# Delta-rule stage of a hybrid encoder layer: values' convolution, q decays and gate product on GpSimd, one-strand substitution

## The chip, the core and the metric

The kernel runs on one core of one Trainium2 chip. Five engines work side by side, each through its own instruction stream in a fixed order: PE (TensorE, matrix products), DVE (VectorE), ACT (ScalarE), POOL (GpSimd) and SP (which issues most DMAs). Semaphores tie the streams together. The metric is the device time of one execution in microseconds. The kernel before takes 1628.24 us (median of 3 runs, 1626.96 to 1631.02).

## The reference, cut to what matters

One layer: a norm, one wide projection, two token mixers in parallel, gates, an output projection. The change lies in mixer A, the gated delta rule, with 8 heads of width 128 over 1024 tokens, in both directions.

```python
qkv_a = silu(centred_depthwise_conv(qkv_a, conv_w))      # 5 taps along the tokens, per channel
q_a, k_a, v_a = split(qkv_a, 3); q_a = l2norm(q_a); k_a = l2norm(k_a)
# gated_delta_rule, per head and direction, in chunks:
diff = g[..., :, None] - g[..., None, :]
decay = where(incl, exp(diff), 0)
lower = where(strict, einsum(kb, k) * decay, 0)          # kb = k * beta
u, w  = triangular_solve(I + lower, [v * beta, kb * exp(g)])
attn  = einsum(q, k) * decay; q_dec = q * exp(g); k_dec = k * exp(g_last - g)
for each chunk:                                          # the scan over chunks
    v_new = u - w @ S
    o     = q_dec @ S + attn @ v_new
    S     = S * exp(g_last) + k_dec.T @ v_new
o_a = rmsnorm(o_fwd + o_bwd) * silu(z_a)                 # z_a: a further part of the projection
```

## The kernel before, in words

**Stages.** First the tokens are normalised and split in two single-precision parts (`hh`, `hl`), so that each projection is three products. Then comes the delta-rule stage over heads h = 0 to 7, then mixer B (GLA, 4 heads), then the two mixer projections (`pj_y`) and the output projection (`pout`). The sixteen gate projections `t0` to `t15` are work for PE that may stand anywhere; thirteen are planned behind the last delta-rule head.

**One head of the delta-rule stage** has four parts:
- `gdn_project(h+1)`: PE computes k, q and v (`pj_a`) and the gate z (`pj_z`) of the next head. ACT copies each result into a padded buffer `xp` (2 of them). The 5-tap convolution is one product with a scalar (L517, for q on ACT at L515) and four multiply-adds on DVE (L519), each over 128x1024. SiLU on ACT follows (L500). z is copied out to DRAM (`z_d`) as it is.
- `gdn_decay(h+1)`: loads the decay exponents, masks them on POOL (L585), takes exponentials on ACT (L588).
- `gdn_inverse(h)`: products k k^T (`pgr`), scaled into `um` (L628). The 32x32 diagonal blocks are inverted by back substitution on DVE (L641 to L653): 31 steps, each a product into `tmp` (L651) and a subtraction from `yl` (L653), done in two strands (even and odd columns), so 4 instructions a step, 120 a head. Then PE joins the blocks (`p1`, `py`, `px`, `p2`, `p3`); the values are turned to token order and scaled (L731, on DVE); the q k^T products are multiplied by the decays (L740).
- `gdn_scan(h)`: 8 chunk steps in both directions, an alternation of small PE products and small DVE and ACT instructions (`r` L780, `vd` L786, `vn` L788, `S` L798, outputs `po` L767). Ahead of it the decays exp(g) are loaded into `qe` and multiplied by q (L749, DVE). Behind it come the norm, the product with silu(z) (`finish`, L472; the multiplication shows as L127 `zs`), two multiply-adds with PSUM (L476) and the store.

**What sets the order.** Instructions are recorded with priorities: the inverse of head h+1 ranks ahead of the scan of head h, the projections rank last and fill PE. A scheduler lays out each engine's stream once, by its own estimate of durations; on the chip every engine then takes its stream strictly in that order. POOL also computes the low parts `lo` of the weights (L184) on which the next projections wait.

**Buffers** in the stage: q 2, k 3, v 3 (`A_BUFS`), `xp` 2, `qe` 2 (used again for the output `o`), one `zs`.

Of the kernel before, what the change touches and what calls it, by code (L numbers as in the profile page):

```python
# [32 lines left out]

WRAW, WSPLIT, XS, XP = 2, 4, 4, 2

A_BUFS = (2, 3, 3)

# [53 lines left out]
def layer_kernel(  # L91
# [107 lines left out]
    for h in range(HA):  # L199
        plan += [(f"a{j}_{h}", w_in, [(j * D + h * P, P, 0)]) for j in A_ORDER]  # L200
        plan.append((f"z{h}", w_in, [(C_Z + h * P, P, 0)]))
        if h > 0:
            plan_gates(("gdn", h - 1), GDN_FILL[h - 1])
    plan_gates(("gdn", HA - 1), GDN_FILL[HA - 1])
    for h in range(HB):
# [192 lines left out]
    SC = [P, 2, HA, NT]  # L398
    be = mconst.tile(SC, F32, name="be")
    nb = mconst.tile(SC, F32, name="nb")  # L400
    ev = mconst.tile([P, 2, 3, HA, NT], F32, name="ev")
    nE = mconst.tile(SC, F32, name="nE")
    def scan_gates(pool):
# [44 lines left out]
        for d in range(2):  # L448
# [49 lines left out]
    def gdn_project(h, pool):  # L498
        a = [pool.tile([P, T], F32, tag=f"a{j}", name=f"{'qkv'[j]}{h}", bufs=A_BUFS[j]) for j in range(3)]
        silu = lambda t: tc.keep_in_program_order(nc.scalar.activation(t, t, AF.Silu))  # L500
        for j in A_ORDER:
            xp = pool.tile([P, T + 4], F32, tag="xp", name=f"xp{j}_{h}", bufs=XP)
            nc.gpsimd.memset(xp[:, 0:2], 0.0)
            nc.gpsimd.memset(xp[:, T + 2:T + 4], 0.0)
            evac = lambda th, ps: nc.scalar.copy(xp[:, 2 + th * 512:2 + th * 512 + 512], ps)
            if h == 0 and j == A_ORDER[0]:
                evac(0, ps_a[0])
                for i in range(2, 4):
                    a_steps[i]()
                evac(1, ps_a[1])  # L510
            else:
                project(f"a{j}_{h}", evac)
            ct = j * 8 + h
            if j == 0:
                nc.scalar.mul(a[j], xp[:, 0:T], cw[:, ct, 0:1])  # L515
            else:
                nc.vector.tensor_scalar(a[j], xp[:, 0:T], cw[:, ct, 0:1], None, op0=ALU.mult)  # L517
            for k in range(1, 5):
                nc.vector.scalar_tensor_tensor(a[j], xp[:, k:k + T], cw[:, ct, k:k + 1], a[j], op0=ALU.mult, op1=ALU.add)  # L519
            if h == 0 and j == A_ORDER[0]:  # L520
                table(SILU)
                silu(a[j])
                exp_ln_table()
        if h == 0:
# [3 lines left out]
            exp_ln_table()  # L528
            with at(P_FILL):
                project_out("z0", z_d[:, 0])  # L530
# [9 lines left out]
    zs = {}  # L540

# [49 lines left out]
    def gdn_inverse(h, pool, sm, qkv, dt):  # L591
        qT, kT, vT = qkv
        t2 = lambda n, shape: pool.tile(shape, F32, tag="t2", name=f"{n}{h}", bufs=4)
# [48 lines left out]
        for i in range(31, 0, -1):  # L642
            for par in range(2):
                s0 = (i // 2 + 1 - par) // 2
                w_ = 8 - s0
                if w_ == 0:
                    continue
                tmp = sm.tile([P, 31 * 8], F32, tag=f"tmp{par}", name=f"tmp{h}_{i}_{par}", bufs=1)
                tv = tmp[:, :i * w_].rearrange("p (r s) -> p r s", s=w_)
                yv = yl.rearrange("p r (s e) -> p e r s", e=2)[:, par, :, s0:]  # L650
                nc.vector.tensor_tensor(tv, ul2[:, i, 0:i].unsqueeze(2).broadcast_to([P, i, w_]),  # L651
                                        yv[:, i].unsqueeze(1).broadcast_to([P, i, w_]), op=ALU.mult)
                nc.vector.tensor_tensor(yv[:, 0:i], yv[:, 0:i], tv, op=ALU.subtract)  # L653
        yt = t2("yt", [P, 16, 32])
# [88 lines left out]
    def gdn_scan(h, pool, sm, qkv, dt, um, ktok, vtok, rk2, c2):  # L743
        qT, kT, _ = qkv
# [24 lines left out]
        for s in range(NT):  # L769
# [30 lines left out]
            for d, n in un:  # L800
# [3 lines left out]
                add_o(n, vn[d], dt[:, d * NT + n])  # L804
        if h == HA - 1:
            zs[h] = gdn_z(h, pool)
            table(SILU)
            tc.keep_in_program_order(nc.scalar.activation(zs[h], zs[h], AF.Silu))
            exp_ln_table()

# [7 lines left out]
    with tc.tile_pool(name="gdn", bufs=1) as pool, tc.tile_pool(name="gdns", bufs=2) as sm:  # L818
        scan_gates(pool)
        o128 = mconst.tile([P, P], F32, name="o128")  # L820
# [4 lines left out]
        for h in range(HA):  # L825
# [327 lines left out]
```

## Time and profile before

| | |
|---|---|
| median of 3 runs | 1628.24 us |
| profiled execution | 1627.11 us, span of its instructions 1624.2 us |
| busy share PE / DVE / ACT / POOL | 94% / 54% / 43% / 12% |
| mean granted clock of PE | 0.961 |
| the chain that ended last | PE 67%, DVE 16%, ACT 7%, DMA 6% |

The span divides at about 80 us and 845 us: start, delta-rule stage, everything later. Busy times are unions of the instructions' durations on an engine. A PE that reads busy is not PE at its peak, since matmuls are pipelined.

### The profile page before, as it was taken

Reading aid. Unit: us, or ns where it says so; the run is one execution under the profiler, and the core shown is the slowest. Engines: PE = TensorE matmul, PEld = TensorE weight load, DVE = VectorE, ACT = ScalarE, POOL = GpSimd, SP = SyncE. Lnnn points to the kernel's source line nnn. Section 1 sums busy time; section 2 is a strip of 40 time slices with the busy share of each in tenths; the row PEclk is TensorE's granted clock in tenths of the full one; section 3 lists DMA queues with packets and bytes.
Section 4 is the critical chain, followed back from the end, with each engine's and each line's share of the span. In section 5 each row is a group of like instructions: output and inputs, shape, how many; then the busy total and the mean of one; then the engine's idle time right before and its main releaser. Section 6 shows DMA issues by size and latency. Waiting matters only on the chain.

```text
span 1624.2 us, 25070 instructions
## 1 busy us (share of the span) xinstructions
PE 1531.2 (94%) x9500; PEld 1290.5 (79%) x9500; DVE 881.9 (54%) x2340; ACT 696.9 (43%) x1473; POOL 193.8 (12%) x207
## 2 busy tenths in 40 slices
PE   6978997998899999999989999999999999899998
PEld 6867776787777878778778888898888988787887
DVE  5486486877879897958541013313314245435413
ACT  5462443355364645543332234524525455424311
POOL 3211131112122121200000020020110100000000
PEclk9988996999999999989899999999999999999999
DMA  5320230112032221312234321131231335755404
GB/s 162 130 67 21 72 97 27 33 66 73 26 111 66 79 91 47 110 53 59 83 104 123 99 71 40 40 98 33 72 71 41 91 97 159 230 161 174 133 32 156
DMA packets 142562, 142.05 MB, mean 87 GB/s; under 512 B 11419, under 2 KB 115531, under 8 KB 141413
## 3 DMA queue, kind: packets, MB, share of 16 engines
q1 hardware_dynamic: 134546, 126.11, 25.9%
q10 hardware_dynamic: 7256, 12.26, 2.5%
q0 software_dynamic: 640, 2.10, 0.4%
q8 instruction: 74, 1.21, 0.3%
q14 instruction: 46, 0.38, 0.1%
HBM read 109.97 MB, written 30.46 MB: 86 GB/s over the span
## 4 chain that ended last, share of the span: by engine, by line
PE 67%; DVE 16%; ACT 7%; DMA 6%; issue 2%; SPq 2%; POOL 1%; DVEq 0%; ACTq 0%; POOLq 0%
PE pj_t L254 9%; PE pj_y L254 8%; PE pj_v L243 6%; PE pout L143 5%; PE pj_a L254 5%; PE pj_g L254 5%; DVE tmp L651 4%; DVE yl L653 4%; PE pj_k L254 3%; PE pj_z L254 3%; PE pj_q L254 2%; PE po L767 2%; PE psb L945 2%; PE pob L967 2%; PE psc L793 2%
## 5 line engine op out<-in xcount | busy, mean ns | idle before, releaser
L254 PE MATMUL pj_a<-hh,hi_a 128*128 128x512 f32 x368 | 154.5, 420 | 11.1 <-ACT gz L284 6.9
L254 PE MATMUL pj_a<-hl,hi_a 128*128 128x512 f32 x368 | 153.2, 416 | 0.0
L254 PE MATMUL pj_a<-hh,lo_a 128*128 128x512 f32 x368 | 152.5, 414 | 0.0
L254 PE MATMUL pj_t<-hh,hi_t 128*128 128x512 f32 x256 | 105.4, 412 | 0.0
L254 PE MATMUL pj_t<-hl,hi_t 128*128 128x512 f32 x256 | 105.0, 410 | 0.0
L254 PE MATMUL pj_t<-hh,lo_t 128*128 128x512 f32 x256 | 104.6, 408 | 0.0
L184 POOL TENSOR_TENSOR lo_a<-raw_a,hi_a 128x512 fp32r<-128x512 f32 x48 | 70.0, 1457 | 281.3 <-ACT hi_a L180 259.1
L788 ACT ACTIVATE vn<-psc,rk 128x128 f32<-128x128 f32 x128 | 45.2, 366 | 120.8 <-DVE vd L786 73.5
L651 DVE TENSOR_TENSOR tmp<-ulb,yl 128x54 f32<-128x54 f32 (+13 forms) x480 | 93.3, 234 | 1.8 <-DMA yl<-in_consts_dram 1.7
L254 PEld LDWEIGHTS pj_a<-hh,hi_a 128*128 128x128 f32 x368 | 72.9, 198 | 25.4 <-ACT gz L284 7.6
L653 DVE TENSOR_TENSOR yl<-yl,tmp 128x54 f32<-128x54 f32 (+13 forms) x480 | 90.9, 231 | 0.1
L254 PEld LDWEIGHTS pj_a<-hl,hi_a 128*128 128x128 f32 x368 | 72.5, 197 | 14.0 <-issue 0.7
L254 PEld LDWEIGHTS pj_a<-hh,lo_a 128*128 128x128 f32 x368 | 72.1, 196 | 13.8 <-issue 0.7
L254 PE MATMUL pj_y<-ob,hi_y 128*128 128x512 f32 x256 | 79.0, 390 | 1.3 <-DVE gb L1072 1.3
L143 PE MATMUL pout<-wo,hh 128*128 128x512 f32 (+1 forms) x272 | 79.7, 377 | 0.0
L243 PE MATMUL pj_v<-lo_v,hh 128*128 128x256 f32 x256 | 72.4, 283 | 0.0
L243 PE MATMUL pj_v<-hi_v,hl 128*128 128x256 f32 x256 | 72.4, 283 | 0.0
L243 PE MATMUL pj_v<-hi_v,hh 128*128 128x256 f32 x256 | 72.4, 283 | 0.0
L184 POOL TENSOR_TENSOR lo_v<-raw_v,hi_v 128x512 fp32r<-128x512 f32 x32 | 41.3, 1291 | 233.0 <-ACT hi_v L180 233.0
L180 ACT CAST hi_a<-raw_a 128x512 fp32r<-128x512 f32 x48 | 29.7, 620 | 67.0 <-PE pj_a L254 38.0
L143 PEld LDWEIGHTS pout<-wo,hh 128*128 128x128 f32 x272 | 50.1, 188 | 9.5
L793 PE MATMUL psc<-vd,ktok 128*128 128x128 f32 x224 | 47.2, 305 | 11.0 <-ACT vn L788 11.0
(315 smaller groups left out, 3993.1 us busy)
## 6 DMA issues: line engine op xcount, KB each, us to landing
raw_a<-in_w_in_dram SPq DMA_DIRECT2D x48, 256.0 KB
dt<-cr_d SPq DMA_DIRECT2D x8, 1024.0 KB
qe<-eg_d SPq DMA_DIRECT2D x16, 512.0 KB
raw_t<-in_w_in_dram SPq DMA_DIRECT2D x32, 256.0 KB
gt_d<-gt SPq DMA_DIRECT2D x64, 128.0 KB
raw_v<-in_w_in_dram SPq DMA_DIRECT2D x32, 256.0 KB
xt<-in_x_dram SPq DMA_DIRECT2D x8, 512.0 KB
raw_z<-in_w_in_dram SPq DMA_DIRECT2D x16, 256.0 KB
```

The lines of the kernel that those rows point to most:

```text
L143: nc.tensor.matmul(ps, lhsT=a(k), rhs=b(k), start=(s == 0), stop=(s == len(steps) - 1))
L180: i = nc.scalar.copy(hi, raw)
L184: nc.gpsimd.tensor_tensor(lo, raw, hi.bitcast(F32), op=ALU.subtract)
L243: nc.tensor.matmul(ps[b][:, c * 256:(c + 1) * 256], lhsT=a[th][:, kk, ts], rhs=w[:, k, :], start=kk == 0 and i == 0 and c == 0, stop=kk == ...
L254: nc.tensor.matmul(ps[:, cols], lhsT=a[:, k, :], rhs=b[th][:, kk, cols], start=kk == 0 and a is hi and b is src[0], stop=kk == KD - 1 and ...
L651: nc.vector.tensor_tensor(tv, ul2[:, i, 0:i].unsqueeze(2).broadcast_to([P, i, w_]), yv[:, i].unsqueeze(1).broadcast_to([P, i, w_]), op=ALU ...
L653: nc.vector.tensor_tensor(yv[:, 0:i], yv[:, 0:i], tv, op=ALU.subtract)
L767: nc.tensor.matmul(po_n(n), lhsT=lhsT, rhs=rhs, start=count[b] == 1, stop=count[b] == len(todo[b]))
L788: nc.scalar.mul(vn[d], pc[d][:, P:2 * P], rk2[:, n:n + 1])
L793: nc.tensor.matmul(pc[d][:, 2 * P:3 * P], lhsT=ktok[:, ns], rhs=vd[d], start=True, stop=True)
L945: nc.tensor.matmul(p_s[:, :256], lhsT=ktok[:, u], rhs=vt[:, n], start=True, stop=True)
L967: nc.tensor.matmul(po[e][:, j * P:(j + 1) * P], lhsT=a, rhs=b, start=(i == 0), stop=(i == len(todo) - 1))
```

## The change

- The convolution of v, for heads 1 to 7, goes to POOL: per half of 512 tokens 5 products with a scalar and 4 additions, 18 instructions a head, with a scratch tile `cv`. The first product of k goes from DVE to ACT.
- The products of q with the decays (`qe`) and the product of the norm factor with the gate go from DVE to POOL.
- The scaling of the values in token order goes from DVE (2 instructions) to ACT (8).
- The substitution has one strand: 2 instructions a step, 62 a head, each over all columns that are still needed.
- z of head h-1 is projected after k, q, v of head h (before: z of head h), and its SiLU is taken before the store to DRAM; it is loaded behind the scan into a `qe` buffer.
- Buffers: k and v share 5, q has 2, `xp` 3. beta is multiplied into the exponentials once.

```diff
-WRAW, WSPLIT, XS, XP = 2, 4, 4, 2
-A_BUFS = (2, 3, 3)
+WRAW, WSPLIT, XS, XP = 2, 4, 4, 3
+Q_BUFS, KV_BUFS = 2, 5
@@ plan
         plan += [(f"a{j}_{h}", w_in, [(j * D + h * P, P, 0)]) for j in A_ORDER]
-        plan.append((f"z{h}", w_in, [(C_Z + h * P, P, 0)]))
         if h > 0:
+            plan.append((f"z{h - 1}", w_in, [(C_Z + (h - 1) * P, P, 0)]))
@@ gdn_project
+            if j == 2 and h > 0:
+                for th in range(2):
+                    nc.gpsimd.tensor_scalar(a[j][:, half(th)], xp[:, th * 512:th * 512 + 512], cw[:, ct, 0:1], None,
+                                            op0=ALU.mult)
+                    for k in range(1, 5):
+                        cv = pool.tile([P, 512], F32, tag="cv", name=f"cv{h}_{th}_{k}", bufs=1)
+                        nc.gpsimd.tensor_scalar(cv, xp[:, th * 512 + k:th * 512 + k + 512], cw[:, ct, k:k + 1], None,
+                                                op0=ALU.mult)
+                        nc.gpsimd.tensor_tensor(a[j][:, half(th)], a[j][:, half(th)], cv, op=ALU.add)
+                continue
+            nc.scalar.mul(a[j], xp[:, 0:T], cw[:, ct, 0:1])
...
-        project_out(f"z{h}", z_d[:, h])
-        zs[h - 1] = gdn_z(h - 1, pool)
+        z = gdn_z(h - 1, pool)
         table(SILU)
-        for t in a + [zs[h - 1]]:
-            silu(t)
+        for j in range(3):
+            silu(a[j])
+        z()
@@ gdn_z (new)
+        def evac(th, ps):
+            for c in range(2):
+                g_ = pool.tile([P, 256], F32, tag="gz", name=f"gz{h}_{th}_{c}", bufs=4)
+                nc.scalar.copy(g_, ps[:, 256 * c:256 * c + 256])
+                parts.append((g_, z_d[:, h, half(th)][:, 256 * c:256 * c + 256]))
+        project(f"z{h}", evac)
+        def end():
+            for g_, dst in parts:
+                tc.keep_in_program_order(nc.scalar.activation(g_, g_, AF.Silu))
+                nc.sync.dma_start(dst, g_)
@@ gdn_inverse
-            for par in range(2):
...
+            w_ = 16 - i // 2
+            tmp = sm.tile([P, 136], F32, tag="tmp", name=f"tmp{h}_{i}", bufs=1)
+            tv = tmp[:, :i * w_].rearrange("p (r s) -> p r s", s=w_)
+            yv = yl[:, :, i // 2:]
...
-            nc.vector.tensor_tensor(by128(vtok[:, half(g)]), by128(pv),
-                                    nk[:, 4 * g:4 * g + 4].unsqueeze(2).broadcast_to([P, 4, P]), op=ALU.mult)
+            for j in range(4):
+                n = 4 * g + j
+                nc.scalar.mul(vtok[:, n * P:(n + 1) * P], pv[:, j * P:(j + 1) * P], nk[:, n:n + 1])
@@ gdn_scan
-            nc.vector.tensor_tensor(qe, qe, qT, op=ALU.mult)
+            nc.gpsimd.tensor_tensor(qe, qe, qT, op=ALU.mult)
...
-        finish([(half(g), po[g]) for g in range(2)], gdn_w[:, 0:1], osq, zs[h], o, oa_d, h)
+        z = pool.tile([P, T], F32, tag="qe", name=f"z{h}", bufs=2)
+        nc.sync.dma_start(z, z_d[:, h])
+        nc.gpsimd.tensor_tensor(z, osq, z, op=ALU.mult)
+        for g in range(2):
+            nc.vector.scalar_tensor_tensor(o[:, half(g)], po[g], gdn_w[:, 0:1], z[:, half(g)], op0=ALU.mult, op1=ALU.mult)
+        nc.sync.dma_start(oa_d[:, h], o)
```

On POOL, around the substitution of head 2, from the load of its start matrix (`yl2`) to the clearing of `xa2`, the tile used right behind it, the stream before reads:

```order
L641 DMA yl2_2975<-in_consts_dram 128x512
L184 TENSOR_TENSOR lo_z3_1_3515<-raw_z3_1_3512,hi_z3_1_3514 128x512
L184 TENSOR_TENSOR lo_a1_4_0_3545<-raw_a1_4_0_3542,hi_a1_4_0_3544 128x512
L184 TENSOR_TENSOR lo_a1_4_1_3584<-raw_a1_4_1_3581,hi_a1_4_1_3583 128x512
L184 TENSOR_TENSOR lo_a0_4_0_3614<-raw_a0_4_0_3611,hi_a0_4_0_3613 128x512
L503 MEMSET xp1_4_4351 128x2
L504 MEMSET xp1_4_4351 128x2
L671 MEMSET xa2_3173 128x512
```

The same place now (L826 is the gate product, L762 the q decays, L517 to L523 the convolution):

```order
L657 DMA yl2_2781<-in_consts_dram 128x512
L826 TENSOR_TENSOR z1_2707<-osq1_2485,z1_2707 128x1024
L184 TENSOR_TENSOR lo_z2_0_3198<-raw_z2_0_3195,hi_z2_0_3197 128x512
...
L762 TENSOR_TENSOR qe0_2_3408<-qe0_2_3408,q2_2157 128x1024
L762 TENSOR_TENSOR qe1_2_3411<-qe1_2_3411,q2_2157 128x1024
...
L517 TENSOR_SCALAR v3_3087<-xp2_3_3232,cw_110 128x512
L521 TENSOR_SCALAR cv3_0_1_3300<-xp2_3_3232,cw_110 128x512
L523 TENSOR_TENSOR v3_3087<-v3_3087,cv3_0_1_3300 128x512
...
L683 MEMSET xa2_2892 128x512
```

Four `lo` stood between the two marks; now a gate product, two q decays, the 18 instructions of head 3's convolution and five `lo` do. Counted so over heads 0 to 6, 53 of the 126 convolution instructions, 6 gate products and 4 q decays stand between these marks (heads 0, 2, 3 and 5 hold the convolutions; in heads 1, 4 and 6 it stands behind them).

On DVE, at the start of head 4's substitution (`tmp4`, `yl4`; `r3`, `vd3`, `S3` belong to the scan of head 3), the stream before:

```order
L651 TENSOR_TENSOR tmp4_31_1_4953<-ulb4_4949,yl4_4951 128x31
L651 TENSOR_TENSOR tmp4_29_0_4959<-ulb4_4949,yl4_4951 128x29
L780 SCALAR_TENSOR_TENSOR r3_0_4_4766<-psc3_0_4_4763,nE_533,v3_3362 128x128
L653 TENSOR_TENSOR yl4_4951<-yl4_4951,tmp4_31_1_4953 128x31
L653 TENSOR_TENSOR yl4_4951<-yl4_4951,tmp4_29_0_4959 128x29
L517 TENSOR_SCALAR k5_5337<-xp1_5_5339,cw_110 128x1024
```

and now:

```order
L663 TENSOR_TENSOR tmp4_31_4641<-ulb4_4637,yl4_4639 128x31
L799 TENSOR_SCALAR vd3_0_2_4404<-psc3_0_2_4395,c2_3_3668 128x128
L665 TENSOR_TENSOR yl4_4639<-yl4_4639,tmp4_31_4641 128x31
L799 TENSOR_SCALAR vd3_1_2_4409<-psc3_1_2_4396,c2_3_3668 128x128
L663 TENSOR_TENSOR tmp4_30_4644<-ulb4_4637,yl4_4639 128x30
L665 TENSOR_TENSOR yl4_4639<-yl4_4639,tmp4_30_4644 128x30
L663 TENSOR_TENSOR tmp4_29_4647<-ulb4_4637,yl4_4639 128x58
```

Where two independent instructions of the substitution followed each other, each now needs the one before it, and instructions of the scan stand between some of them.

## Rows read from the trace of the kernel before

**Rows 1.** Busy time by stretch, all engines (columns in the first line).
```profile
core 0: us, PE busy (x) PEld busy (x) DVE busy (x) ACT busy (x) POOL busy (x), PEclk, DMA share, GB/s
...
80.00:845.00 765.00, 701.12 (x5033) 583.27 (x5032) 575.90 (x1837) 355.54 (x816) 114.96 (x129) 0.92 0.22 67
845.00:1624.00 779.00, 765.55 (x4064) 649.13 (x4062) 264.95 (x449) 300.58 (x581) 52.57 (x46) 1.00 0.35 102
```
**Rows 2.** Waits of PE, 80 to 845 us: total us, times, longest.
```profile
PE p L682 <- DVE xq L661: 18.4, 4, 8.6
...
PE po L767 <- DVE qe L749: 3.1, 1, 3.1
```
**Rows 3.** The chain that ended last, 80 to 845 us, by line.
```profile
by line: PE pj_a L254 8.5%; DVE tmp L651 8.3%; DVE yl L653 8.0%; PE pj_z L254 5.4%; PE po L767 5.1%; PE pj_t L254 4.2%; issue 3.7%; PE psc L793 3.2%; PE psc L778 2.9%; PE psc L783 2.9%; ACT dt L588 2.4%; PE py L691 2.4%; DVE k L519 2.1%; PE
```
**Rows 4.** Groups on DVE, 80 to 845 us: busy us, mean ns | idle before.
```profile
L519 DVE SCALAR_TENSOR_TENSOR v<-xp,cw,v 128x1024 f32<-128x1024 f32 x32 | 43.3, 1352 | 0.1
...
L519 DVE SCALAR_TENSOR_TENSOR k<-xp,cw,k 128x1024 f32<-128x1024 f32 x28 | 37.6, 1342 | 0.0
...
L749 DVE TENSOR_TENSOR qe<-qe,q 128x1024 f32<-128x1024 f32 x16 | 20.4, 1274 | 16.7 <-ACT q L500 13.7 <-DMA qe<-eg_d 2.8
...
L731 DVE TENSOR_TENSOR v<-pv,nk 128x512 f32<-128x512 f32 x16 | 10.8, 689 | 6.7 <-ACT nk L724 3.4 <-PE pv L730 3.0
L127 DVE TENSOR_TENSOR zs<-osq,zs 128x1024 f32<-128x1024 f32 x7 | 10.5, 1495 | 6.1 <-ACT osq L490 6.0
...
L517 DVE TENSOR_SCALAR v<-xp,cw 128x1024 f32<-128x1024 f32 x8 | 8.1, 1017 | 3.6 <-ACT xp L505 3.6
...
L517 DVE TENSOR_SCALAR k<-xp,cw 128x1024 f32<-128x1024 f32 x7 | 5.8, 833 | 7.3 <-ACT xp L505 7.3
```
**Rows 5.** The substitution's own instructions (tile yl) in its eight stretches, last and sum.
```profile
739.90:762.50 22.60, 16.41 (x120) 0.00 (x0) 1.00 0.22 59
sum 238.30, DVE 156.75 POOL 0.00; mean DVE 19.59 POOL 0.00
```
**Rows 6.** All engines in the same eight stretches, last and sum.
```profile
739.90:762.50 22.60, 22.42 (x130) 18.97 (x128) 22.25 (x145) 5.63 (x14) 0.00 (x0) 1.00 0.22 59
sum 238.30, PE 215.91 PEld 177.68 DVE 228.48 ACT 67.47 POOL 44.27; mean PE 26.99 PEld 22.21 DVE 28.56 ACT 8.43 POOL 5.53
```
**Rows 7.** Line L651: duration ns, minimum, median, maximum.
```profile
L651 DVE TENSOR_TENSOR tmp<-ulb,yl x480: 156/208/1345, 104.6 to 762.0; 128x28 f32<-128x28 f32 x32, 128x50 f32<-128x50 f32 x24, 128x64 f32<-128x64 f32 x16, 128x65 f32<-128x65 f32 x16
```
**Rows 8.** Timeline of DVE from 129 us: start us, duration us.
```profile
130.09 0.59 DVE L655 COPY yt<-yl 128x512 f32<-128x512 f32 x1
130.71 0.71 DVE L657 STREAM_TRANSPOSE ytb<-yt 128x512 f32<-128x512 f32 x1
```
**Rows 9.** Timeline of DVE, 662.5 to 666 us.
```profile
662.48 0.38 DVE L653 TENSOR_TENSOR yl<-yl,tmp 128x69 f32<-128x69 f32 x2
662.78 1.24 DVE L651 TENSOR_TENSOR tmp<-ulb,yl 128x66 f32<-128x66 f32 x2
663.94 2.40 DVE L653 TENSOR_TENSOR yl<-yl,tmp 128x66 f32<-128x66 f32 x2
```
**Rows 10.** Timeline of POOL, 661 to 667 us.
```profile
662.76 2.23 POOL L585 TENSOR_SCALAR_AFFINE_SELECT dt<-dt 128x1024 f32<-128x1024 f32 x2 [8.75 <-DMA dt<-cr_d]
664.96 1.29 POOL L184 TENSOR_TENSOR lo_a<-raw_a,hi_a 128x512 fp32r<-128x512 f32 x1
```
**Rows 11.** Groups on POOL, whole span.
```profile
L184 POOL TENSOR_TENSOR lo_v<-raw_v,hi_v 128x512 fp32r<-128x512 f32 x32 | 41.3, 1291 | 233.0 <-ACT hi_v L180 233.0
...
L585 POOL TENSOR_SCALAR_AFFINE_SELECT dt<-dt 128x1024 f32<-128x1024 f32 x16 | 21.1, 1347 | 39.9 <-DMA dt<-cr_d 29.0 <-PE pk L602 10.9
L349 POOL TENSOR_TENSOR xs<-xt,wpre 128x1024 f32<-128x1024 f32 x4 | 11.2, 2790 | 8.1 <-DMA xt<-in_x_dram 8.1
...
L671 POOL MEMSET xa<- 128x512 f32 x8 | 4.7, 588 | 66.2 <-PE pj_t L254 47.1 <-DVE ytb L657 19.1
```
**Rows 12.** Groups on ACT, 80 to 845 us.
```profile
L788 ACT ACTIVATE vn<-psc,rk 128x128 f32<-128x128 f32 x128 | 45.2, 366 | 120.8 <-DVE vd L786 73.5 <-PE psc L783 20.2 <-DVE tmp L651 14.1
```

More of the change, by code (lines that the diff above doesn't have):

```diff
@@ L398, in layer_kernel @@
     SC = [P, 2, HA, NT]
[L399 to L402, printed above, removed]
     def scan_gates(pool):
@@ L440, in scan_gates @@
         nc.vector.scalar_tensor_tensor(fl(lb), fl(ab[:, 2:4]), 0.0, fl(lb), op0=ALU.min, op1=ALU.subtract)
+        be = v4(part(tc_, 2, 1))
         nc.scalar.activation(be, lb, AF.Exp)
@@ L498, in gdn_project @@
     def gdn_project(h, pool):
-        a = [pool.tile([P, T], F32, tag=f"a{j}", name=f"{'qkv'[j]}{h}", bufs=A_BUFS[j]) for j in range(3)]
+        a = {j: pool.tile([P, T], F32, tag="kv" if j else "q", name=f"{'qkv'[j]}{h}", bufs=KV_BUFS if j else Q_BUFS)
+             for j in A_ORDER}
         silu = lambda t: tc.keep_in_program_order(nc.scalar.activation(t, t, AF.Silu))
@@ L528, in gdn_project, with gdn_z @@
             exp_ln_table()
-            with at(P_FILL):
-                project_out("z0", z_d[:, 0])
-            return a
-        project_out(f"z{h}", z_d[:, h])
-        zs[h - 1] = gdn_z(h - 1, pool)
+            return a
+        z = gdn_z(h - 1, pool)
         table(SILU)
-        for t in a + [zs[h - 1]]:
-            silu(t)
+        for j in range(3):
+            silu(a[j])
+        z()
         exp_ln_table()
         return a
-    zs = {}
+    def gdn_z(h, pool):
+        parts = []
+        def evac(th, ps):
[8 more added lines that the diff above has]
+                nc.sync.dma_start(dst, g_)
+        return end
     def gla_stacks(pool):
@@ L591, in gdn_inverse @@
     def gdn_inverse(h, pool, sm, qkv, dt):
-        qT, kT, vT = qkv
+        qT, kT, vT = (qkv[j] for j in range(3))
         t2 = lambda n, shape: pool.tile(shape, F32, tag="t2", name=f"{n}{h}", bufs=4)
@@ L642, in gdn_inverse @@
         for i in range(31, 0, -1):
-            for par in range(2):
[L644 to L653, printed above, removed]
+            w_ = 16 - i // 2
+            tmp = sm.tile([P, 136], F32, tag="tmp", name=f"tmp{h}_{i}", bufs=1)
+            tv = tmp[:, :i * w_].rearrange("p (r s) -> p r s", s=w_)
+            yv = yl[:, :, i // 2:]
+            nc.vector.tensor_tensor(tv, ul2[:, i, 0:i].unsqueeze(2).broadcast_to([P, i, w_]),
+                                    yv[:, i].unsqueeze(1).broadcast_to([P, i, w_]), op=ALU.mult)
+            nc.vector.tensor_tensor(yv[:, 0:i], yv[:, 0:i], tv, op=ALU.subtract)
         yt = t2("yt", [P, 16, 32])
@@ L743, in gdn_scan @@
     def gdn_scan(h, pool, sm, qkv, dt, um, ktok, vtok, rk2, c2):
-        qT, kT, _ = qkv
+        qT, kT = qkv[0], qkv[1]
         qes = []
@@ L804, in gdn_scan @@
                 add_o(n, vn[d], dt[:, d * NT + n])
[L805 to L809, printed above, removed]
         o = pool.tile([P, T], F32, tag="qe", name=f"o{h}", bufs=2)
@@ L815, in gdn_scan @@
         rs_of(osq, None, o128, "eq", f"a{h}", ((psc, "s0"), (psc, "s1")))
-        finish([(half(g), po[g]) for g in range(2)], gdn_w[:, 0:1], osq, zs[h], o, oa_d, h)
+        z = pool.tile([P, T], F32, tag="qe", name=f"z{h}", bufs=2)
[4 more added lines that the diff above has]
+        nc.sync.dma_start(oa_d[:, h], o)
     with tc.tile_pool(name="gdn", bufs=1) as pool, tc.tile_pool(name="gdns", bufs=2) as sm:
+        nb, nE = (pool.tile(SC, F32, name=n) for n in ("nb", "nE"))
+        ev = pool.tile([P, 2, 3, HA, NT], F32, name="ev")
         scan_gates(pool)
@@ L835, in layer_kernel @@
             with at(P_FILL + P_HEAD * (h + 1)):
+                if h == HA - 1:
+                    z = gdn_z(h, pool)
+                    table(SILU)
+                    z()
+                    exp_ln_table()
                 gates(("gdn", h))
```

14 lines of the change are left out of this document (3 added, 11 removed).

## The prediction

> **What bounds the kernel now.** I read the busy times by stretch first. Behind 845 us PE is busy 766 of 779 us at the full clock, and DVE only 265 [rows 1]: nothing there is touched, and since all PE work stays, the change can gain only in the delta-rule stage, 80 to 845 us. There PE reads busy for 701 of 765 us at a mean granted clock of 0.92 of full speed. So 64 us are idle, and 0.08 x 765 = 61 us of full-speed work are lost to the lower of PE's two levels (1.2 instead of 2.4 GHz), which stands behind stretches in which PE idled. About 125 us is all that can be won. In the same stage DVE is busy 576 us (75%), ACT 356 us, POOL 115 us (15%). DVE is the loaded engine beside PE, POOL the empty one.
>
> The waits of PE come second. The longest in total is for `xq`, the end of the substitution: 18.4 us in four waits [rows 2]. The chain third: 16.3% of the stage, 125 us, is the substitution's two lines, of the 157 us for which they are busy, so about 80% of it stands on the chain. The convolution of k has 2.1%, 16 us of 43, so 37% [rows 3 to 5]. Time on DVE costs the kernel between 37 and 80% of itself, by where it lies.
>
> **What leaves DVE.** Durations are of the rows in the stage [rows 4]. Values' convolution: 7 heads x (4 x 1.352 + 1.017) = 45.0 us. First product of k: 7 x 0.833 = 5.8. Decays on q: 20.4. Gate product: 8 x 1.495 = 12.0. Scaling of the values: 10.8. Together 94 us, of 576. By the 37 to 80% above this is worth 35 to 75 us on the path. The convolutions rank last on DVE and are hidden the most, but they fill the gaps between other heads' work and delay what stands behind them in the stream; the gate product and the decays stand between one scan and the next. I take 0.6: 56 us.
>
> **The substitution with one strand.** In head 7, where POOL does nothing, its 120 instructions keep DVE busy 16.4 us [rows 5, 6], 0.137 us each, though one takes 0.156 at least and 0.208 at the median [rows 7]: two strands overlap. With one, each of the 62 waits for the one before. A dependent pair on DVE shows a gap of 130.71 - 130.68 = 0.03 us [rows 8]. The elements stay the same: 2 x 2856, summed over the steps, at about 1.04 ns (the 128x512 product takes 0.689 us, less 0.156, over 512 elements [rows 4]). So 62 x (0.156 + 0.03) + 5.9 = 17.4 us when it runs alone, 1.0 us more a head. Where instructions of the scan stand between, the gaps cost nothing: then 62 x 0.137 + 5.9 = 14.4, 2.0 less. Over 8 heads -16 to +8 us; I take +5, since the stream has such neighbours only at some steps.
>
> **What POOL does to DVE.** This is the term that decides. At 662.76 us POOL starts two maskings and then a `lo`. In that time DVE's substitution, which does two instructions in 0.38 us elsewhere, needs 1.24 us for two and then 2.40 for two [rows 9, 10]: each is held until a POOL instruction ends, one DVE instruction for one of POOL. Over the eight stretches the substitution is busy 156.8 us instead of 8 x 16.4 = 131.3, so 25.5 us are lost in this way to 44.3 us of POOL work, 0.58 for each us [rows 5, 6].
>
> The Trainium skill states it as a rule ("SBUF — State Buffer", section "SBUF: two separate sides"): VectorE and GpSimd share one port pair, and a GpSimd instruction and a VectorE instruction with two SBUF inputs exclude each other for the whole of an instruction. Read strictly, every us of POOL beside the substitution costs DVE a full us; the rows give 0.58. The strict reading is a rival below.
>
> Added POOL work: a 128x512 addition at 1.291 us [rows 11]; a product with a scalar is not in the trace, between 0.588 (clearing 128x512) and 0.67 (half a masking), I take 0.6. A head's convolution is 8 x 1.291 + 10 x 0.6 = 16.3 us. The 128x1024 products are 2.58 (twice 1.291) to 2.79 each, three a head, 7.7 us. In all 7 x 16.3 + 8 x 7.7 = 176 us, which brings POOL to 291 of 765 us, so it does not become the bound by itself. By the order of its stream, 53 of the 126 convolution instructions, 6 gate products and 4 decays stand beside a substitution: 53 x 0.905 + 10 x 2.58 = 74 us, at 0.58 a stall of 43 us. The other 102 us lie beside scans and block products, where DVE's instructions mostly take one operand from PSUM; only the convolutions of k and q take both from SBUF there. No row shows that case alone; between 0 and 0.58 I take 0.12, nearer to 0 since in heads with convolutions behind the substitution the scan is what stands there: 12 us.
>
> On the path: the substitution's 5 + 43 us at 80% are 38 us, the 12 us at 37% are 4. Against the 56 us won, 14 us remain.
>
> **The small terms.** ACT gains 64 scalings of 0.366 us [rows 12], 23 us, and one product a head; at 356 of 765 us it hides them, and DVE's decays of the q k^T products run beside the scalings. If that cover fails, it costs 64 x 0.366 - 10.8 = 13 us; I take 0. The gate product and two decays on POOL take 7.7 us instead of 4.0 a head, behind whatever POOL holds then, and the output's two `qe` buffers come free only behind the gate; the scan's `po` waits for them and holds PE's stream. PE waited 3.1 us for `qe` in all [rows 2], so there is cover, how much is not in the trace; 0 to 8 x 3.7 = 30 us, I take 4. A third `xp` buffer, and z behind the three convolutions, free the projections from DVE's convolutions: at most what PE waits there, I take -8, bounded by 0 and half of PE's 64 idle us. The SiLU of z and its DMA now stand behind SiLU of v, which waits for POOL; SP's weight loads are queued behind that store. Four converted halves and two raw ones, about 6 x 5.5 = 33 us of PE work by the scheduler's order, lie ready then: 0.
>
> Sum: -56 + 38 + 4 + 0 + 4 - 8 = -18 us on the profiled 1627.1 us: 1609 us. The median of the runs lies 1.1 us above that execution, which I neglect.
>
> **The rivals.**
> Lockstep, slower. Place: POOL's convolution beside the substitution and, at 0.58, beside the k and q convolutions. Then DVE loses 74 + 0.58 x 102 = 133 us and with the strand 138, against 94 that leave. On the path 0.8 x 79 + 0.37 x 59 = 85 us against 56: +29, and with the `qe` wait at +4 and -8 for the projections +25, 1652 us. It decides from the point where DVE pays over (94 - 5) / 176 = 0.51 us for each us of added POOL work; my forecast has 55 / 176 = 0.31. For it: the two rows in lockstep, and 54 POOL instructions a head pressing one after another. Against it: 0.58, not 1, in the trace, and half as many DVE instructions to be held.
>
> Full relief. The convolution slips beside the scans, since the streams shift against each other; 15 us of stalls in all. Then -75 x 0.9 + 8 - 8 = -68, 1559 us, more than half of the 125. For it: POOL at 38%. Against it: the order puts four of seven convolutions beside a substitution.
>
> No change. What leaves DVE was hidden, and the projections, the finish of a scan and the next load of `qe` hold the pace; relief at 37% is 35 us, against 42 of cost and -8: within 3 us of 1627.
>
> **How the numbers follow.** Forecast (1590 to 1622) 0.47, lockstep 0.31, full relief 0.11, no change 0.11. A measurement of this kernel tells some 0.3%, 5 us, from no change. Faster by that: 0.45 + 0.11 = 0.56; within: 0.11 and 0.02 from the forecast's edge, 0.13; slower 0.31. The range reaches to both outer cases, 1563 to 1653; the forecast's own is 1590 to 1622.
>
> **What would show it.** DVE busy in the stage falls from 576 to about 536 us if the terms hold (94 off, 55 to 60 back); at over 570 lockstep has won, below 510 full relief. The substitution's instructions, 62 of them: a median of some 0.24 us, with maxima of 1.3 and 2.6 us; 20 us a head in heads 1, 4 and 6, 27 or more in 0, 2, 3 and 5. POOL at about 290 us, 16 to 20 a convolution. Waits of PE for `xq` should not exceed the 18.4 us by much; if they double, POOL's work beside the substitution costs more than taken. Waits of PE's `po` for the decays on POOL, over 10 us, would show the buffers of `qe` as the new wait. Idle of PE and clock behind 845 us unchanged. The forecast is wrong if the stage ends later than 845 us with DVE less busy: then the cost is in a wait and not in DVE's load.

## The result, and the profile after

The changed kernel takes 1707.96 us (median of 4 runs, 1703.62 to 1724.42) against 1627.6 us: a ratio of 1.051, 95% interval 1.044 to 1.058. It is 80 us slower; the forecast was 18 us faster, and the range ended at 1653. The profiled execution has a span of 1706.8 us, 82.6 more than before.

Busy time by stretch, after (same columns as [rows 1]; the stage now ends at about 925 us):

```profile
80.00:925.00 845.00, 712.27 (x5041) 589.76 (x5040) 550.48 (x1285) 383.72 (x916) 351.32 (x282) 0.88 0.21 62
925.00:1706.00 781.00, 768.52 (x4060) 651.59 (x4058) 261.83 (x445) 299.05 (x579) 52.42 (x44) 0.99 0.34 99
```

All of it lies in the stage: 845 us instead of 765. PE is idle for 133 us there instead of 64 and reads busy 11 us longer, at a mean clock of 0.88 instead of 0.92. DVE does less than before in a longer stage (550 us, before 576): the cost is in PE's waits and in its clock. PE's waits in the stage, after (total us, times, longest):

```profile
PE p L694 <- DVE xq L673: 73.2, 8, 21.4
PE pj_t L255 <- ACT gt L285: 20.5, 5, 9.9
PE py L703 <- DVE p1s L697: 14.7, 4, 5.6
```

The wait for `xq`, the end of the substitution, is 73.2 us over all eight heads, against 18.4 us in four [rows 2]. PE's wait for `qe` is gone. The groups behind it, after, first the substitution on DVE, then four groups of POOL (busy us, mean ns | idle before):

```profile
L665 DVE TENSOR_TENSOR yl<-yl,tmp 128x126 f32<-128x126 f32 (+22 forms) x248 | 94.5, 381 | 5.4
L663 DVE TENSOR_TENSOR tmp<-ulb,yl 128x126 f32<-128x126 f32 (+22 forms) x248 | 94.1, 380 | 7.5 <-DMA yl<-in_consts_dram 2.0
```
```profile
L521 POOL TENSOR_SCALAR cv<-xp,cw 128x512 f32<-128x512 f32 x56 | 89.5, 1598 | 8.0 <-ACT xp L506 4.0 <-ACT nk L736 0.2
L523 POOL TENSOR_TENSOR v<-v,cv 128x512 f32<-128x512 f32 x56 | 73.9, 1320 | 3.8
...
L762 POOL TENSOR_TENSOR qe<-qe,q 128x1024 f32<-128x1024 f32 x16 | 40.5, 2536 | 25.5 <-DMA qe<-eg_d 12.8 <-DVE yl L665 8.1 <-ACT q L501 4.3
L517 POOL TENSOR_SCALAR v<-xp,cw 128x512 f32<-128x512 f32 x14 | 24.6, 1756 | 5.1 <-ACT xp L506 5.0
```

The additions are as before [rows 11], but a product with a scalar takes 1.6 us, not the 0.6 assumed, so a convolution lasts 29 to 35 us and POOL is busy 351 us. The substitution's own instructions in its eight stretches, last and sum (as [rows 5]):

```profile
815.00:840.50 25.50, 18.00 (x62) 0.00 (x0) 0.96 0.48 145
sum 299.30, DVE 188.53 POOL 0.00; mean DVE 23.57 POOL 0.00
```

The stretches last 299 us instead of 238 and hold 188.5 us of the substitution's work instead of 156.8. Lines from head 2 show what POOL's convolution does to it, DVE first, then POOL (start us, duration us; for the kernel before see [rows 9, 10]):

```profile
342.04 0.65 DVE L665 TENSOR_TENSOR yl<-yl,tmp 128x110 f32<-128x110 f32 x1
342.72 0.29 DVE L663 TENSOR_TENSOR tmp<-ulb,yl 128x126 f32<-128x126 f32 x1
343.05 0.29 DVE L665 TENSOR_TENSOR yl<-yl,tmp 128x126 f32<-128x126 f32 x1
343.37 0.28 DVE L663 TENSOR_TENSOR tmp<-ulb,yl 128x120 f32<-128x120 f32 x1
343.69 1.26 DVE L665 TENSOR_TENSOR yl<-yl,tmp 128x120 f32<-128x120 f32 x1
344.99 0.76 DVE L663 TENSOR_TENSOR tmp<-ulb,yl 128x133 f32<-128x133 f32 x1
```
```profile
341.83 1.61 POOL L521 TENSOR_SCALAR cv<-xp,cw 128x512 f32<-128x512 f32 x1
343.52 1.29 POOL L523 TENSOR_TENSOR v<-v,cv 128x512 f32<-128x512 f32 x1
344.91 1.56 POOL L521 TENSOR_SCALAR cv<-xp,cw 128x512 f32<-128x512 f32 x1
```

During the addition one DVE instruction is held to its end (1.26 us instead of 0.28). During the product with a scalar DVE loses some 0.4 us at its start and then passes three instructions. Below, "held" is the time by which the substitution's instructions last longer than the shortest of the same shape in that kernel, summed over all heads: 37 us before, 69 after.

### The profile page after: what moved, and what is told of

Its sections match the earlier page's. It is cut to its first block, busy times and chain, and to the rows that moved or that the text cites. A ratio compares the mean times of both kernels' runs of the same rounds, so it can differ in the third digit from the quotient of the medians.

```text
span 1706.8 us, 24762 instructions
## 1 busy us (share of the span) xinstructions
PE 1544.8 (91%) x9500; PEld 1298.7 (76%) x9500; DVE 852.2 (50%) x1785; ACT 720.6 (42%) x1566; POOL 430.1 (25%) x357
## 4 chain that ended last, share of the span: by engine, by line
PE 57%; DVE 8%; DMA 5%; ACT 4%; POOL 2%; issue 1%; SPq 1%; DVEq 0%; ACTq 0%; POOLq 0%
PE pj_t L255 7%; PE pj_y L255 7%; PE pj_v L244 5%; PE pout L143 5%; PE pj_g L255 4%; PE pj_a L255 4%; PE pj_z L255 3%; PE pj_k L255 3%; PE pj_q L255 2%; DVE yl L665 2%; PE po L780 2%; PE psb L965 2%; PE pob L987 2%; DVE tmp L663 1%; PE psc L806 1%
## 5 line engine op out<-in xcount | busy, mean ns | idle before, releaser
L184 POOL TENSOR_TENSOR lo_a<-raw_a,hi_a 128x512 fp32r<-128x512 f32 x48 | 64.8, 1349 | 222.3 <-ACT hi_a L180 165.9
L663 DVE TENSOR_TENSOR tmp<-ulb,yl 128x126 f32<-128x126 f32 (+22 forms) x248 | 94.1, 380 | 7.5 <-DMA yl<-in_consts_dram 2.0
L665 DVE TENSOR_TENSOR yl<-yl,tmp 128x126 f32<-128x126 f32 (+22 forms) x248 | 94.5, 381 | 5.4
L521 POOL TENSOR_SCALAR cv<-xp,cw 128x512 f32<-128x512 f32 x56 | 89.5, 1598 | 8.0 <-ACT xp L506 4.0
L694 PE MATMUL p<-xq,um 32*32 32x32 f32 x256 | 13.2, 232 | 73.2 <-DVE xq L673 73.2
L523 POOL TENSOR_TENSOR v<-v,cv 128x512 f32<-128x512 f32 x56 | 73.9, 1320 | 3.8
L255 PEld LDWEIGHTS pj_t<-hh,hi_t 128*128 128x128 f32 x256 | 49.5, 193 | 32.5 <-ACT gt L285 22.6
```

The source lines that it names most:

```text
L184: nc.gpsimd.tensor_tensor(lo, raw, hi.bitcast(F32), op=ALU.subtract)
L255: nc.tensor.matmul(ps[:, cols], lhsT=a[:, k, :], rhs=b[th][:, kk, cols], start=kk == 0 and a is hi and b is src[0], stop=kk == KD - 1 and ...
L521: nc.gpsimd.tensor_scalar(cv, xp[:, th * 512 + k:th * 512 + k + 512], cw[:, ct, k:k + 1], None, op0=ALU.mult)
L523: nc.gpsimd.tensor_tensor(a[j][:, half(th)], a[j][:, half(th)], cv, op=ALU.add)
```

## The experiments

Times are medians; ratios are against the kernel before, run on the same chip. On the chips used its own median lies between 1623.5 and 1629.3 us, so a difference of under some 6 us between two experiments says nothing.

**Parts undone (e1, e6, e7, e5).** e1 has the convolution of v back on DVE, its first product on ACT:

```diff
-            if j == 2 and h > 0:
-                for th in range(2):
...
-                continue
```


> The changed kernel with one part undone: values' convolution back on DVE (its first product on ACT, as for k and q). Theory 1, the convolution on POOL: in the changed kernel it takes 27 to 34 us a head instead of the 16 of the prediction, and the waits for xq rose from 18 to 73 us; without it the 80 us come back, 1600 to 1645 us, with xq waits under 30 us. Theory 2, the substitution with one strand is what makes xq late: it stays in this kernel, xq waits stay above 55 us and the time above 1680. Theory 3, the other work moved to POOL (q decays, gate product, z order): 1680 as well, but with xq waits near 20 us.

1660.6 us, 1.021 (1.017 to 1.025); xq waits 35.3 us. Some 35 of the 80 us remain: no theory's number. e6 puts decays and gate product back on DVE too:

```diff
-            nc.gpsimd.tensor_tensor(qe, qe, qT, op=ALU.mult)
+            nc.vector.tensor_tensor(qe, qe, qT, op=ALU.mult)
...
-        nc.gpsimd.tensor_tensor(z, osq, z, op=ALU.mult)
+        nc.vector.tensor_tensor(z, osq, z, op=ALU.mult)
```


> The changed kernel with all three products that went to POOL back on DVE (convolution, q decays, gate product); one strand, order of z, ACT scaling and buffers as changed. Theory A: the strand remains, 1640 to 1660, as with the convolution alone on DVE (1661) less up to 15 us. Theory B: 1615 to 1635.

1611.7 us, 0.990 (0.987 to 0.993): below the ranges of both theories, faster than before and the best of all kernels. The whole loss goes when the three products leave POOL. e7 has two strands in addition:

```diff
+            for par in range(2):
+                s0 = (i // 2 + 1 - par) // 2
...
```


> As the run before, and with two strands again: what is left of the change is the order of z, ACT's scaling of the values and first product of k, and the buffers. Both theories: 1615 to 1635; over 1645 the rest of the change would have a cost of its own, which neither has.

1635.9 us, 1.005 (1.001 to 1.008). e5 is the kernel before with the one-strand substitution alone (the reverse edit):

> The kernel before with the one-strand substitution alone. Theory A, the stream laid out beforehand: PE's products p stand in its stream where the scheduler expected xq, so time that the substitution takes beyond that becomes a wait of PE with half the clock behind it; one strand lengthens the stretch by scan and convolution instructions between its dependent steps, in all heads: 1640 to 1660, xq waits 30 us or more in 6 to 8 waits. Theory B, the strand is cheap and only POOL's load costs: 1620 to 1635, xq waits under 25 us.

1641.3 us, 1.011 (1.004 to 1.019), xq waits 32.8 us in 8: Theory A. So the strand costs 14 us alone (by the interval 6 to 30), and e6 with it is 24 us faster than e7 without it (15 us faster than e18, below, in which the order of e7 is put right). Its own instructions in head 7 take 15.5 us, less than before (16.4 [rows 5]); the stretches grow (28 to 43 us in head 2) since other DVE work stands in its gaps. e3, the changed kernel with the two strands of e7:

> The changed kernel with two strands in the substitution again. Theory 1: twice as many DVE instructions can be held by POOL's, so not faster than the changed kernel by more than 10 us: 1695 to 1720. Theory 2: most of the loss goes, below 1660. Theory 3: 1690 to 1710.

1744.6 us, 1.071 (1.065 to 1.077): slower still, as Theory 1 had it, but by more.

**POOL alone (e2, e8, e9).** e2 is the kernel before with the convolution of v moved from DVE to POOL as in the diff, 18 instructions a head, without the rest of the change.

> The kernel before with values' convolution alone on POOL (heads 1 to 7; two strands, decays and gate product on DVE as before; beta is multiplied into the exponentials once to make room). By its order the convolution stands beside the substitution in heads 1 and 4 only. Theory 1: 1680 to 1710 us, almost the whole loss. Theories 2 and 3: within 10 us of before, 1615 to 1640, since one convolution of three left DVE.

1707.4 us, 1.050 (1.045 to 1.055): Theory 1, the whole loss without strand, decays or gate product. In e8 the convolution stays on DVE, and POOL does as much work that nobody uses:

```diff
+                cv = pool.tile([P, 512], F32, tag="cv", name=f"cv{h}", bufs=1)
+                nc.gpsimd.tensor_scalar(cv, xp[:, 0:512], cw[:, ct, 0:1], None, op0=ALU.mult)
+                for i in range(17):
...
```


> The kernel before with 18 POOL instructions a head added for nothing (10 products with a scalar, 8 additions over 128x512, on a scratch tile; nobody waits for the result), values' convolution still on DVE. By its order 57 of the 126 stand beside a substitution. It prices POOL's presence without the wait of ACT's SiLU for it. If the hold of DVE by POOL is the larger part of the loss of the convolution alone on POOL (+82): 1670 to 1710. If the convolution's own length, behind which SiLU and ACT's stream stand, is the larger part: 1635 to 1655.

1704.1 us, 1.047 (1.039 to 1.054), though nobody waits for the result: with this work in POOL's stream, and the streams laid out for it, the kernel takes 77 us more. e9 is the changed kernel with the two lines of e6 alone:

> The changed kernel with the q decays and the gate product back on DVE; the convolution stays on POOL. Against the kernel with nothing of this on POOL (1612) it prices the convolution alone with one strand. Theory A (POOL's convolution holds DVE and fills POOL's queue, whatever else stands there): 1670 to 1700, xq waits 50 us or more. Theory B (convolution, decays and gate product are dear only together): 1620 to 1650.

1700.5 us, 1.046 (1.043 to 1.050), xq waits 60.5 us: Theory A, at the upper end of its range.

**Convolution left out (e4).**

```diff
             if j == 2 and h > 0:
-                for th in range(2):
...
+                nc.scalar.mul(a[j], xp[:, 0:T], cw[:, ct, 0:1])
                 continue
```

> The changed kernel with four of the five taps of values' convolution left out in heads 1 to 7 (only the first product is taken, on ACT), so neither DVE nor POOL has that work. Theory 1: as with the convolution on DVE or better, 1580 to 1630 us, and the difference to that kernel (expected 0 to 30 us) is what DVE's relief was worth at most. Theories 2 and 3: above 1670.

1702.7 us, 1.048 (1.043 to 1.052): against Theory 1, in the range of Theories 2 and 3, though e6 keeps the strand and the order of z without loss. Its streams were laid out anew, with 14 decays and gate products wholly beside a substitution instead of 10; held are 66.5 us, nearly as after (68.9). What this layout costs shows below (e17).

**Queues (e11, e12): not borne out.** In e8's trace SP stands for 31.8 us at loads of raw weights, whose buffers POOL's `lo` frees only behind the idle work. A store of z stands behind these loads, ACT has no free buffer `gz` until it is done, and PE waits 14 us for ACT:

```profile
237.34 31.80 SPq L177 DMA_DIRECT2D raw_a<-in_w_in_dram  x4
```
```profile
273.03 0.80 PE L254 MATMUL pj_a<-hh,hi_a 128*128 128x512 f32 x1 [14.14 <-ACT gz L284]
```

e12 moves that store; e11 moves, in the changed kernel, the stores and the clearing of `xa` (its edit is shown):

```diff
-                nc.sync.dma_start(dst[:, half(th)][:, 256 * c:256 * c + 256], g_)
+                nc.scalar.dma_start(dst[:, half(th)][:, 256 * c:256 * c + 256], g_)
...
-        nc.gpsimd.memset(xa, 0.0)
+        nc.vector.memset(xa, 0.0)
```


> The kernel before with the idle POOL work (1704), and the stores of z issued by ACT instead of SP. There SP, in order, waited 32 us with a load of raw weights for POOL's lo, which stood behind the idle work; the store of z behind that load came late, so ACT had no buffer, and PE waited 14 us. Theory A, queues: PE's waits for gz fall from 28 to under 10 us, 1665 to 1690. Theory B, the hold of DVE: 1695 to 1710.

> The changed kernel, with the work that stood behind the convolution in a queue moved to another: the clearing of xa on DVE instead of POOL, the stores of z and of the gate projections issued by ACT instead of SP. Theory A, queues (what stood on POOL and SP before is now late): the waits of py (14.7 us) and of pj_t for gt (20.5 us) go, 1665 to 1690. Theory B, the hold of DVE is all: 1700 to 1715.

e12: 1707.1 us, Theory B's time; the wait for gz fell from 28 to 14 us and the time not at all. e11: 1733.5 us, 1.067 (1.063 to 1.072), above both theories; the waits for `py` and `gt` went as expected (4.5 us left for py), and others came (`pj_a` for `xp` 19.6 us instead of 6.9). Freeing these queues gained nothing; POOL's own queue, with `lo` behind the work, was not freed.

**Masking moved (e10).** One DVE instruction ties the next head's masking to xq:

```diff
+            nc.vector.scalar_tensor_tensor(dt[:, ::NT, 0:1], last_xq[0][:, 0:2, 0:1], 0.0, dt[:, ::NT, 0:1],
+                                           op0=ALU.mult, op1=ALU.add)
```


> The kernel with nothing of this change on POOL (1612), and the masking of the next head's decays, 2.1 us on POOL which stood in the last steps of the substitution, made to wait for xq (one small DVE instruction a head ties them). In the trace of that kernel PE waits 2.1 us for xq in each head and has half its clock for some 10 us behind it. Theory A, the hold by POOL makes this wait: it goes, and 2 to 7 us a head with it, 1565 to 1600. Theory B, the substitution is late by itself: the wait stays at 2 us and the time within 1605 to 1620.

1647.2 us, 1.013 (1.009 to 1.018): both miss. The substitution's stretch fell from 38.2 to 36.1 us, but PE's stream was laid out anew too. PE waits 2.2 us as in e6, and has half its clock for 23.9 us behind it instead of 13.7 (head 3; the half clock, then the whole period; columns as [rows 1]):

```profile
427.10:451.00 23.90, 23.90 (x229) 19.93 (x227) 10.41 (x15) 14.82 (x34) 2.27 (x4) 0.50 0.22 67
383.10:478.60 95.50, 90.63 (x619) 76.24 (x618) 65.31 (x168) 52.58 (x117) 14.31 (x19) 0.86 0.21 64
```

So here less hold (21.6 us instead of 36.7) went with the same wait and 35 us more time: a new layout, or the later masking, is worth as much as a part of the change.

**The order (e13 to e16).** In the changed kernel's DVE stream the substitution of heads 2, 5 and 7 stands wholly behind the scan of the head before: the two no longer overlap. These heads take 129, 108 and 113 us, the others about 90. e13 ranks the SiLU first:

```diff
+        with at(P_HEAD * (h + 1) + 5000):
             table(SILU)
```


> The changed kernel with one priority changed: the SiLU of the next head's q, k, v ranks ahead of the scan instead of last. By its order every substitution then stands inside the scan of the head before (in the changed kernel that of heads 2, 5 and 7 stands wholly behind it); all POOL work stays. Theory 1, lost overlap: three periods of 108 to 129 us fall to 90 to 96, time 1625 to 1660. Theory 2, POOL's hold of DVE, with PE's waits for xq and the half clock behind them: 1690 to 1715.

1691.7 us, 1.039 (1.034 to 1.043): Theory 2; the overlap came back in all heads, but only 16 us with it. e14 is e6 with a later inverse:

```diff
-P_Y = 10000
+P_Y = 16000
```

> The kernel with nothing of this change on POOL (1612), with one constant changed so that the inverse of the next head ranks behind the scan: by its order nearly all substitutions then stand behind the scan of the head before. Theory 1: every period of 89 us grows to 105 to 125, time 1725 to 1860. Theory 2: without POOL work the order costs little, since the projections fill PE: 1612 to 1650.

1659.9 us, 1.020 (1.015 to 1.025), 10 us above Theory 2 and far below Theory 1: seven lost overlaps cost 48 us. e15 and e16 are e2 and the kernel before with the edit of e13:

> The kernel before with the convolution alone on POOL (1707), and the SiLU ranked first as in the changed kernel's variant. By its order the overlap that two heads had lost (periods of 116 and 112 us) is there again, and the convolution stands beside the substitution in one head and parts of three. Theory 1: 1645 to 1670. Theory 2: 1695 to 1715.

> The kernel before with the SiLU ranked first alone; it shows what that priority gives without POOL work. By its order one lost overlap comes back (head 6, period 93 us). Theory 1: 0 to 15 us faster than before, 1612 to 1628. Theory 2: no difference that can be measured, 1623 to 1632.

e15: 1694.9 us; e16: 1623.5 us, 0.997 (0.994 to 0.999). So the order is worth some 12 to 16 us where the convolution is on POOL. It is not always so little: e4 has the overlap lost in heads 2 and 5 (131 and 107 us), and the same edit in it (e17, below) gives 47 us. The order is a part of the loss and not all of it, since e13, with every overlap back, is still 80 us above e6.

**The regular pair, and the dose (e17, e18).** e6 and e13 repeat one pattern in nearly every head, so one head shows the price. e6, head 3: from the substitution's last step to PE's first product on xq, PE's half clock, the rest, the whole period (columns as [rows 1]):

```profile
403.90:409.40 5.50, 3.38 (x20) 2.48 (x19) 5.43 (x9) 3.10 (x11) 0.53 (x1) 1.00 0.01 1
409.40:423.10 13.70, 13.70 (x175) 11.51 (x172) 9.83 (x15) 6.55 (x17) 3.65 (x4) 0.50 0.47 155
423.10:454.40 31.30, 30.07 (x217) 25.81 (x217) 13.44 (x40) 26.96 (x58) 4.58 (x5) 1.00 0.18 51
365.70:454.40 88.70, 84.62 (x619) 70.81 (x618) 65.06 (x168) 52.19 (x116) 14.90 (x19) 0.92 0.22 69
```

And e13, head 3, with the substitution's stretch in a row ahead of these:

```profile
400.00:443.00 43.00, 36.69 (x203) 30.29 (x203) 41.46 (x104) 17.82 (x41) 16.84 (x15) 1.00 0.19 64
443.00:446.30 3.30, 0.00 (x0) 0.00 (x0) 3.13 (x6) 0.74 (x2) 0.52 (x1) 0.50 0.92 272
446.30:470.00 23.70, 23.68 (x247) 20.11 (x248) 5.97 (x10) 6.42 (x15) 21.55 (x14) 0.50 0.09 27
470.00:499.10 29.10, 28.91 (x167) 23.78 (x165) 13.98 (x42) 21.03 (x54) 8.63 (x10) 1.00 0.22 64
400.00:499.10 99.10, 89.27 (x616) 74.18 (x616) 64.55 (x160) 45.99 (x111) 47.54 (x39) 0.86 0.20 62
```

PE's first product on xq, in e6 and then in e13:

```profile
409.23 1.43 PE L684 MATMUL p<-xq,um 32*32 32x32 f32 x29 [2.12 <-DVE xq L663]
```
```profile
446.32 1.56 PE L695 MATMUL p<-xq,um 32*32 32x32 f32 x29 [8.22 <-DVE xq L674]
```

The substitution takes 43.1 us instead of 38.2, 4.9 more, since POOL is beside it for 17 us instead of 6. PE waits 8.2 us instead of 2.1, and then does the block products at half the clock until 470 us, 27 us in all instead of 14. The period grows by 10.4 us: 5.8 of idle time (99.1 - 89.3 against 88.7 - 84.6) and 4.6 of PE that reads busy longer. So 1 us by which the substitution lasts longer goes with 2.1 us of the period; the pair differs in the place of the SiLU as well. e17 takes the convolution out of e13 as e4 does out of the changed kernel:

> The changed kernel with the SiLU first (1692), and four of the five taps of values' convolution left out in heads 1 to 7, so that neither DVE nor POOL has them; decays and gate product stay on POOL. Theory 1, hold: the five convolution instructions in the last steps of each substitution (7.2 us of POOL, held at about 0.49 of it, 3.5 us) go, and 2.1 times that a head: 1630 to 1650, xq waits of 3 to 5 us a head in place of 8. Theory 2, the wait for xq is made by the order and not by the hold: 1680 to 1695.

1655.9 us, 1.016 (1.010 to 1.023): nearer to Theory 1, 6 us above its range; the waits for xq are 43.2 us in eight, 5.4 to 5.5 in six of them, not 3 to 5. The substitution of head 3:

```profile
386.00:426.30 40.30, 36.83 (x204) 30.31 (x203) 38.73 (x104) 17.82 (x41) 9.57 (x10) 1.00 0.18 60
```

Against e13, which has the convolution on POOL and else the same edit, the stretch is 2.7 us shorter and the kernel 36 us faster, 5.1 for each of seven heads: 1.9 for each us. e18 is e7 with the edit of e13:

> Two strands, nothing of this change on POOL (1636 with two lost overlaps), and the SiLU first, by whose order every substitution stands inside the scan before. Theory 1: two strands end the substitution some 10 us earlier than one (28 against 38 us), PE finds xq ready, the half clock behind it goes: 1580 to 1605, and below the best so far (1612). Theory 2: with two strands the scan's instructions wait instead: 1612 to 1635.

1626.5 us, 1.002 (0.999 to 1.006): Theory 2. PE finds xq ready (one wait of 7.2 us), but waits 27.4 us for the scan's `vn` (22.6 in e7).

Held time and median, over the kernels with one strand that differ in POOL's work: e6 36.7 and 1612; e17 43.5 and 1656; e1 51.5 and 1661; e9 58.3 and 1701; e13 62.1 and 1692; e4 66.5 and 1703; after 68.9 and 1708. From the first to the last 3 us of time go with each us held, but between neighbours it is -2.3 to 6.5, and kernels outside this list do not follow it: e10 (21.6 and 1647) and e5 (36.6 and 1641) are slower than e6 with no more held. Held time is one part of the loss, the layout of the streams another.

## Why the prediction was wrong, step by step

**What bounds the kernel**: right. Nothing changed behind the stage, and PE's idle time and clock carry the whole difference.

**What leaves DVE, 94 us at 0.6 = -56**: the first step that failed. In e17 the convolution is on no engine, in e1 on DVE; decays and gate product are on POOL in both, the overlap is complete in both. e17 is 4.7 us faster, for 28 multiply-adds of 1.53 us, 43 us, less on DVE. That is about 0.1 of the work; by the two intervals it lies between nothing and 0.45, not at 0.6. (e17 also has the SiLU first, which made no kernel slower that it was tried in, and so hides no gain. The other 49 us that leave DVE were not measured by themselves.) The share on the chain had been taken from lines that stand last on it, the substitution's, and lent to work that fills the gaps between them. DVE at 75% was not what PE waited for; one chain on it was.

**Substitution with one strand, +5**: alone it costs 14 us (e5; 6 to 30), above the bounds of -16 to +8, and for another reason: not the gaps cost, but what the stream puts into them. Beside the rest it gains.

**What POOL does to DVE, a stall of 43 + 12 us**: the size was nearly right, 69 - 37 = 32 us held in the substitution, and 11 in the convolutions of k and q (busy for 83.0 us against e6's 71.5). Two errors cancel in it: products with a scalar take 1.6 us instead of 0.6, but hold DVE only 0.33 us each, additions 1.0 of their 1.3, the gate product 2.1 of 2.4 (means over the instructions wholly beside the substitution, in after and e13). The rule of the Trainium skill ("SBUF — State Buffer", section "SBUF: two separate sides") that both engines exclude each other for a whole instruction nearly fits the latter two, and not the product with a scalar.

**Its weight on the path, 0.8**: the second step that failed. The end of the substitution is followed by PE's block products; what is late there goes with PE's wait and half the clock behind it, about twice the delay in the regular pairs. e1 against e6, which differ only in decays and gate product and overlap in all heads, shows more: beside the substitution the gate product holds the last steps for 15 us in seven heads, and with the decays on POOL the kernel takes 49 us more. PE idles 94 us instead of 79 and reads busy 38 us longer for the same work, at a lower clock (whole span, e6 and then e1; columns as [rows 1]):

```profile
0.00:1700.00 1700.00, 1530.47 (x9500) 1291.58 (x9500) 830.84 (x1837) 760.00 (x1598) 184.15 (x207) 0.96 0.28 84
0.00:1700.00 1700.00, 1568.14 (x9500) 1323.72 (x9500) 822.57 (x1813) 761.90 (x1598) 237.80 (x231) 0.93 0.28 84
```

Line by line in e1, DVE first, then POOL:

```profile
421.85 2.36 DVE L655 TENSOR_TENSOR yl<-yl,tmp 128x45 f32<-128x45 f32 x1
424.24 0.19 DVE L653 TENSOR_TENSOR tmp<-ulb,yl 128x30 f32<-128x30 f32 x1
```
```profile
421.73 2.42 POOL L816 TENSOR_TENSOR z<-osq,z 128x1024 f32<-128x1024 f32 x1
```

**The two steps together.** For the move of the three products to POOL the terms are -46 (77 us at 0.6), +39 (43 us at 0.8 and 12 at 0.37) and +4 (the wait for `qe`): -3 us. From e6 to after it costs 96. Part of this is the overlap lost in three heads, for which the sum had no term.

**Markers.** DVE 550 us in the stage (536 forecast), POOL 351 (290), a convolution 29 to 35 us (16 to 20), `xq` 73 us (18): DVE's load came near the forecast, the wait did not, and the stage ended later with DVE less busy, as written for a cost that sits in a wait.

**Small terms.** ACT at 0 holds (384 us of 845). The wait for `qe`, +4, did not come. The xp and z order, -8, cannot be separated: all but POOL and the strand is +8 (e7).

**The rivals.** Lockstep had the side and the place, not the mechanism: it wanted over 0.51 us of hold for each us of added POOL work; 43 us for some 236 us (351 - 115) are 0.18. "No change" had the relief as hidden, but still at 37%. That a delay counts double, and that the layout loses overlap, was in none of them.

**The sum as measured**, from e6: -16 for all that is not on POOL (1611.7 - 1627.6) and +96 for the three products on POOL (after - e6), together +80. How the 96 divide depends on the way, since each step lays the streams out anew:
- By e17 and e13: +44 for decays and gate product (e17 - e6, with the convolution off DVE as well), +36 for the convolution (e13 - e17), +16 for the lost overlap of three heads (after - e13).
- By e17 and e4: +44, then +47 for the order (e4 - e17), then +5 for the convolution (after - e4).
- One group alone: +89 for the convolution (e9 - e6), so decays and gate product on top of it add 7.

**Open.** Why e10's half clock lasts longer behind the same wait. Why the idle work in e8 costs 77 us with only 18 us more held, and the convolution 71 us in e15 (against e16) with 10 us more held (45.3 against 34.9): in these kernels with two strands the hold of the substitution is not shown to be the main cost. What else is late was seen in e8's waits, but taking one of them away (e12) gave nothing. How the loss divides between hold and layout stays open.

## What to carry to other kernels

Price a delay where it ends: at a point where PE waits and starts small products, a late microsecond went with two to three here, while work taken from the gaps of a busy engine gave about a tenth, and less than half, of its time. Before work is moved to GpSimd, look at what VectorE does beside it, and above all at the last steps before a wait of TensorE. Where a scheduler lays out the streams, count in the order how many heads still overlap, and price a part in more than one layout: the same convolution was worth 36 us in one and 5 in another.

## What the runs showed of the hardware

A product of 128x512 with a scalar on GpSimd takes 1.57 us at the median, longer than the addition of two such tiles (1.27), and lets VectorE's two-input instructions pass after some 0.4 us. An addition held one of them for 1.0 of its 1.3 us, a masking of 128x1024 for 0.8 of 1.1 (e6). GpSimd work whose result nobody uses slowed the kernel by 4.7% (e8), its streams laid out anew.
